# Two gate chunks at a time, half of their rows as seven block products

## The chip, the cores and the metric

The kernel runs on one NeuronCore of a Trainium2 chip. The core has five engines that run their own instruction queues in order: TensorE (PE, matrix products; its weight loads are listed apart as PEld), VectorE (DVE), ScalarE (ACT), GpSimd (POOL) and SyncE (SP, which here only issues transfers). Data lie in SBUF, 128 partitions wide; TensorE writes its sums to PSUM, eight banks of 128 x 512 float32. Transfers between HBM and SBUF run on 16 DMA engines. The metric is the device time of one execution in microseconds; lower is better.

## The reference, cut to what matters

One layer of a streaming encoder for 256 tokens of 2048 features, in float32. The part that the change touches is the mixer:

```python
proj = h @ w_in                                   # h: 256 x 2048
(rq, rk, rv, rg, gqkv, ga, gb, gz, gate_a, gate_b) = split(proj)
yr = groupnorm(retention(rope(rq), rope(rk), rv))
yr = silu(rg) * yr
yg = rmsnorm(gated_delta_rule(conv_silu(gqkv), ga, gb))
yg = silu(gz) * yg
merged = sigmoid(gate_a) * yr + sigmoid(gate_b) * yg
x = x + merged @ w_out
```

After it come cross-attention and an MLP. `rg`, `gz`, `gate_a` and `gate_b` are each 256 x 2048 = h times a 2048 x 2048 slice of `w_in`; these four products are the gate chunks.

## The kernel before, in words

**Products in two parts.** Every float32 operand of a matmul is split into a rounded half and a remainder, `hi` and `lo`, and a product is three matmuls: hi x hi, hi x lo, lo x hi. The activations h are split once (`h1`, four quads of 512 features each, a quad holding `hi` and `lo` of 4 x 128 features by 256 tokens). Weights are split as they arrive: SP loads 1 MB into `raw` (three buffers), ScalarE rounds 1024 columns of it into `whi` (L124), VectorE subtracts into `wlo` (L125). So one load is two halves, each a `whi`/`wlo` pair of 128 x 1024; there are three buffers of each. TensorE frees a buffer with its last matmul on it.

**Chunks.** A chunk (`chunk`) is 512 output columns for all 256 tokens: two PSUM tiles (128 tokens each, t = 0 and 1) from `stream_ps`, four loads (q = 0..3, 512 rows of the weights each), 4 x 4 x 2 x 3 = 96 matmuls with the activations as weights and 512 columns of `whi`/`wlo` moving (L169 to L171). Then `evac` reads the PSUM tiles: for the gates ScalarE takes silu or tanh into `gth` (L931) and VectorE multiplies into `yr` or `yg` (L937, L943).

**Groups.** The mixer runs in four groups j = 0..3 (a quarter of the features each). The main loop goes: `gdn_stream(j)` (twelve block loads, convolution, Gram matrices in `kh`/`kl`), `gdn_blocks(j)` (a triangular solve of 31 small steps on VectorE in `lw` and `tw`, stored and reloaded as `ct`), the delta-rule gates of group j-1 (`of_delta_rule`: GZ then TB), `retention(j)` (q, k, and the chunk V, scores, norm of `yr`), then the retention gates of group j (`of_retention`: RG then TA). `gdn_core(j)` is a generator of eight small steps on TensorE, VectorE, ScalarE and GpSimd; `step()` lets it go on by one between the parts of a chunk. For j > 0 it runs during the retention gates. In the fifth pass only the delta-rule gates of group 3 are left, and `take_back` splits the merged results of the first three groups in between, into the places of the quads of h that are no longer needed.

**Order.** The program's order on each engine comes from a planner that lays the instructions out by their dependencies and priorities against its own timeline; `high_priority` lifts the weight loads and splits over everything else, the gates' `evac` less far, and `issue_after` pins an instruction behind another one. On the chip each engine's queue then runs in that fixed order.

**PSUM.** Four of the eight banks belong to the chunks (`s0`, `s1`, two each), the other four are handed out in turn by `bank()` for scores, Gram matrices, transposes and the core's steps.

**A form of sums.** The MLP's second product (`with_seven`, L1232 and L1266) already computes half of its rows in blocks of two by two, as seven block products of 12 matmuls instead of eight. Sums and differences of the weights' blocks are made on VectorE (L1266), those of the activations once per group.

Of the kernel before, what the change touches and what calls it, by code (L numbers as in the profile page):

```python
# [54 lines left out]
def trunk(ctx: ExitStack, tc: tile.TileContext, x_f, mem_f, positions, lead_f, small_f, w_blocks, w_chunks, w_ga,  # L55
# [15 lines left out]
        s1 = psp.tile([P, 512], F32, name="s1", tag="s1", bufs=2)  # L71
        return s0, s1

    def bank():
        return psp.tile([P, 512], F32, name="b", tag="b", bufs=4)


    fetched, steps, latest = [], [], {}
# [587 lines left out]
    def gdn_stream(grp):  # L666
# [3 lines left out]
        for pr in range(2):  # L670
# [17 lines left out]
                r4 = mx.tile([P, 4, NT, GD], F32, name="r4", tag="r4", bufs=1)  # L688
            grams = []
            ssk, ssq = (mx.tile([P, 2, NT], F32, name=nm, tag=nm, bufs=2) for nm in ("ssk", "ssq"))  # L690
            for b in range(2):
                kh = mx.tile([P, 2, S], F32R, name="kh", tag="kh", bufs=2)
                kl = mx.tile([P, 2, S], F32R, name="kl", tag="kl", bufs=2)
                act.activation(kh, kq[:, b], AF.Copy)
                vec.tensor_sub(kl, kq[:, b], kh.bitcast(F32))
                g0, g1 = bank(), bank()
                g0v = g0.rearrange("p (a n) -> p a n", a=2)
                g1v = g1[:, 0:256].rearrange("p (a n) -> p a n", a=2)
                for n, (l, r) in enumerate(((kh, kh), (kh, kl), (kl, kh))):
                    pe.matmul(g0v, l[:, 0, 0:P], r, start=n == 0, stop=n == 2)  # L700
                for n, (l, r) in enumerate(((kh, kh), (kh, kl), (kl, kh))):
                    pe.matmul(g1v, l[:, 0, P:S], r[:, :, P:S], start=n == 0, stop=n == 2)
                grams.append((g0v, g1v))
                for t, src in enumerate((g0v[:, 0, 0:P], g1v[:, 0, :])):
                    dj = sm.tile([P, S], F32, name="dj", tag="bo", bufs=2)[:, :P]
                    vec.scalar_tensor_tensor(dj, src, 1.0, ident, op0=ALU.mult, op1=ALU.mult,
                                             accum_out=ssk[:, b, t:t + 1])
# [217 lines left out]
            vec.tensor_mul(yr[:, t, :], yr[:, t, :], gng)  # L925


    def gates():
        def gate_of(ps, f, scale):
            th = mx.tile([P, 512], F32, name="gth", tag="gth", bufs=1)  # L930
            act.activation(th, ps, f, scale=scale)  # L931
            return th

        def silu_gate(y):
            def evac(t, ps, c0, c1):
                th = gate_of(ps, AF.Silu, 1.0)
                vec.scalar_tensor_tensor(y[:, t, :], th, 0.5, y[:, t, :], op0=ALU.mult, op1=ALU.mult)  # L937
            return evac

        def sig_gate(y, other=None):  # L940
            def evac(t, ps, c0, c1):
                th = gate_of(ps, AF.Tanh, 0.5)
                vec.scalar_tensor_tensor(y[:, t, :], th, 1.0, y[:, t, :], op0=ALU.add, op1=ALU.mult)  # L943
                if other is not None:
                    vec.tensor_add(y[:, t, :], y[:, t, :], other[:, t, :])
            return evac

        def of_retention(j, yr):
            chunk(h1, cols(w_chunks, H_RG + j), silu_gate(yr))
            chunk(h1, cols(w_chunks, H_TA + j), sig_gate(yr))  # L950

        def of_delta_rule(j, yr, yg, quad, before=None):
            chunk(h1, cols(w_chunks, H_GZ + j), silu_gate(yg))
            chunk(h1, cols(w_chunks, H_TB + j), sig_gate(yg, yr), before=before, cuts=2 if before else 1)
            to_feature(lambda t, f: yg[:, t, f * P:(f + 1) * P], quad)

        return of_retention, of_delta_rule
# [10 lines left out]
    gate_retention, gate_delta_rule = gates()  # L968
    for j in range(5):
        if j < 4:  # L970
            heads, cmp_l, r4, qe4 = gdn_stream(j)
            solved = gdn_blocks(heads, cmp_l)
        if j:
# [511 lines left out]
```

## Time and profile before

| | us |
|---|---|
| median of 3 runs | 2043.6 (2042.51 to 2044.07) |
| the profiled execution | 2043.71 |
| its span, first to last instruction | 2042.0 |
| TensorE busy | 2030.0 |
| VectorE busy | 1564.4 |
| ScalarE busy | 1202.4 |
| GpSimd busy | 39.5 |
| mean DMA rate | 198 GB/s |

A row of the profile names line, engine, operation, written and read tiles, shape and count, then busy time, the mean of one in ns, and idle time before with what ended it. Busy times of TensorE are those of overlapping matmuls: each is followed from its start to its modelled end, and the next one has started long before. How fast TensorE goes is seen in the distances between starts. Stretches are in us from the span's start; the mixer's groups lie between about 270 and 1060 us.

### The profile page before, as it was taken

Reading aid. Unit: us, or ns where it says so; the run is one execution under the profiler, and the core shown is the slowest. Engines: PE = TensorE matmul, PEld = TensorE weight load, DVE = VectorE, ACT = ScalarE, POOL = GpSimd, SP = SyncE. Lnnn points to the kernel's source line nnn. Section 1 sums busy time; section 2 is a strip of 40 time slices with the busy share of each in tenths; the row PEclk is TensorE's granted clock in tenths of the full one; section 3 lists DMA queues with packets and bytes.
Section 4 is the critical chain, followed back from the end, with each engine's and each line's share of the span. In section 5 each row is a group of like instructions: output and inputs, shape, how many; then the busy total and the mean of one; then the engine's idle time right before and its main releaser. Section 6 shows DMA issues by size and latency. Waiting matters only on the chain.

```text
span 2042.0 us, 28478 instructions
## 1 busy us (share of the span) xinstructions
PE 2030.0 (99%) x10790; PEld 1751.2 (86%) x10790; DVE 1564.4 (77%) x2427; ACT 1202.4 (59%) x1979; POOL 39.5 (2%) x50
## 2 busy tenths in 40 slices
PE   9999999999999999999999999999999999999998
PEld 8888888988888888888888899888888888888886
DVE  5887788779668875788567666777887887888788
ACT  5665764575457554755446565566557656656655
POOL 0000000000000000000000000000000000000000
PEclk9999999999999999999999999999999999999999
DMA  8678556455545554555467554568636546555661
GB/s 328 210 267 290 182 185 201 157 187 193 188 170 181 193 194 164 182 188 194 146 211 251 196 176 158 183 216 277 208 130 238 215 159 220 196 203 174 238 228 62
DMA packets 79642, 405.24 MB, mean 198 GB/s; under 512 B 16512, under 2 KB 24592, under 8 KB 34832
## 3 DMA queue, kind: packets, MB, share of 16 engines
q1 hardware_dynamic: 79072, 402.74, 57.4%
q8 instruction: 84, 1.38, 0.3%
q10 hardware_dynamic: 432, 0.69, 0.1%
q14 instruction: 54, 0.44, 0.1%
HBM read 389.74 MB, written 11.55 MB: 197 GB/s over the span
## 4 chain that ended last, share of the span: by engine, by line
PE 97%; DVE 2%; issue 0%; DMA 0%; ACT 0%; DVEq 0%; POOLq 0%; POOL 0%; ACTq 0%
PE s L213 52%; PE s L170 8%; PE s L171 8%; PE s L169 8%; PE s L1232 7%; PE b L1232 7%; PE s L402 1%; PE s L403 1%; PE s L404 1%; PE b L797 1%; PE b L700 1%; PE b L141 1%; PE b L830 1%; PE b L140 1%; PE b L142 1%
## 5 line engine op out<-in xcount | busy, mean ns | idle before, releaser
L213 PE MATMUL s<-q,whi 128*128 128x512 f32 x2824 | 971.6, 391 | 0.0
L125 DVE TENSOR_TENSOR wlo<-raw,whi 128x1024 fp32r<-128x1024 f32 x599 | 730.5, 1222 | 284.0 <-ACT whi L124 279.4
L124 ACT ACTIVATE whi<-raw 128x1024 fp32r<-128x1024 f32 x599 | 635.0, 1061 | 500.2 <-PE s L213 219.1
L213 PE MATMUL s<-q,wlo 128*128 128x256 f32 x2824 | 766.1, 281 | 0.0
L213 PEld LDWEIGHTS s<-q,whi 128*128 128x128 f32 x2824 | 521.8, 188 | 100.9
L213 PEld LDWEIGHTS s<-q,wlo 128*128 128x128 f32 x2824 | 528.7, 188 | 13.1 <-DVE wlo L125 0.4
L170 PE MATMUL s<-wlo,q 128*128 128x512 f32 x704 | 277.2, 394 | 0.0
L171 PE MATMUL s<-whi,q 128*128 128x512 f32 x704 | 274.9, 391 | 0.0
L169 PE MATMUL s<-whi,q 128*128 128x512 f32 x704 | 254.4, 391 | 0.0
L169 PEld LDWEIGHTS s<-whi,q 128*128 128x128 f32 x704 | 132.1, 188 | 27.3
L171 PEld LDWEIGHTS s<-whi,q 128*128 128x128 f32 x704 | 132.3, 188 | 26.3
L170 PEld LDWEIGHTS s<-wlo,q 128*128 128x128 f32 x704 | 132.3, 188 | 26.2
L222 ACT ACTIVATE bo<-s 128x256 f32<-128x256 f32 x192 | 73.3, 382 | 109.4 <-PE s L213 109.2
L1232 PE MATMUL s<-whi,q 128*128 128x512 f32 x384 | 122.1, 389 | 0.0
L223 DVE TENSOR_TENSOR bo<-bo,s 128x256 f32<-128x256 f32 x192 | 79.9, 416 | 41.9 <-ACT bo L222 41.5
L1255 DVE TENSOR_TENSOR wlo<-rt,whi 128x1024 fp32r<-128x1024 f32 x55 | 67.4, 1226 | 35.8 <-ACT whi L1254 35.4
L213 PE MATMUL s<-q,whx 128*128 128x512 f32 x248 | 86.6, 390 | 0.0
L1232 PEld LDWEIGHTS s<-whi,q 128*128 128x128 f32 x384 | 72.1, 188 | 14.9
L1254 ACT ACTIVATE whi<-rt 128x1024 fp32r<-128x1024 f32 x55 | 58.2, 1059 | 41.8 <-PE s L1232 29.4
L1232 PE MATMUL s<-wlo,q 128*128 128x512 f32 x192 | 74.7, 389 | 0.0
L213 PE MATMUL s<-q,wlx 128*128 128x256 f32 x248 | 68.2, 280 | 0.0
L1232 PE MATMUL b<-whi,q 128*128 128x512 f32 x208 | 67.2, 389 | 0.0
(355 smaller groups left out, 2328.2 us busy)
## 6 DMA issues: line engine op xcount, KB each, us to landing
raw<-w_ff SPq DMA_DIRECT2D x96, 1024.0 KB
raw<-w_chunks SPq DMA_DIRECT2D x79, 1024.0 KB
raw<-w_blocks SPq DMA_DIRECT2D x64, 1024.0 KB
raw<-w_xk SPq DMA_DIRECT2D x16, 1024.0 KB
raw<-w_out SPq DMA_DIRECT2D x16, 1024.0 KB
raw<-w_xq SPq DMA_DIRECT2D x16, 1024.0 KB
raw<-w_xo SPq DMA_DIRECT2D x16, 1024.0 KB
rt<-w_ff SPq DMA_DIRECT2D x16, 1024.0 KB
```

Source lines behind the costliest of these rows:

```text
L124: latest["hi"] = act.activation(hi[:, cs], src[:, cs], AF.Copy).ins
L125: latest["lo"] = vec.tensor_sub(lo[:, cs], src[:, cs], hi[:, cs].bitcast(F32)).ins
L140: pe.matmul(o, lhs[0], rhs[0], start=first, stop=False)
L169: pe.matmul(o, xh, wh, start=first, stop=False)
L170: pe.matmul(o, xh, wl, start=False, stop=False)
L171: pe.matmul(o, xl, wh, start=False, stop=last)
L213: ins = pe.matmul(ps[b][:, :S] if part else ps[b], halves[h][part][:, i, b * P:(b + 1) * P], x[:, kk % 4, :], start=kk == 0 and not part, ...
L222: act.activation(o, ps[b][:, S:], AF.Copy)
L223: vec.tensor_add(o, o, ps[b][:, :S])
L1232: ins = pe.matmul(o, lhs[l], rhs[r], start=key not in opened, stop=last and j == 2, skip_group_check=True).ins
L1254: latest["hi"] = act.activation(hi, raw[:, c:c + 1024], AF.Copy).ins
L1255: latest["lo"] = vec.tensor_sub(lo, raw[:, c:c + 1024], hi.bitcast(F32)).ins
```

## The change

The gates keep their values, but four pairs of chunks are computed together by a new function, `two_chunks`: the retention gates (RG and TA) of groups 1, 2 and 3, and the delta-rule gates (GZ and TB) of group 3. Of the 2048 rows, quads 2 and 3 (`plain`) are computed as before. Rows of quads 0 and 1 are taken as a product of blocks: tokens in two halves of 128, rows in two halves of 512, and the two chunks as the two halves of the columns. Seven products of 12 matmuls (`product`) take the place of eight.

The sums on the side of the tokens are made once, into `s_in` (`sums_of_tokens`, hung into `turns`, so that they are issued after the 10th, 20th, 30th and 40th half from the start of group 1). The sums on the side of the weights are made in SBUF: x takes the block (chunk 1, quad 0) by two plain loads, VectorE adds b11 (`add_to`), GpSimd issues two transfers that add the block (1, 1) from HBM on top (`add_parts`, `accum_op`), and later two that add (0, 1); y takes (1, 0) and VectorE adds b22. Three partial sums are kept in `u` and `d` (places of `vh` and `vl`), and the gates' `evac` adds them (`more`) before the silu or tanh.

In the order of the code a pair is eleven parts: plain(0, 2), b11, x, plain(0, 3), b22, x, plain(1, 2), b21, y, x, plain(1, 3). x lies in the places of `kq` and `lw`, y in those of `qk` and `tw`. The four turning banks become two tags of two banks, `b` and `c`; during a pair `c` holds `shared` and `p5`, and the core's steps have `b` alone. The tiles `kh`, `kl` of the Gram matrices move to the places of `vh` and `vl`. The scratch space for transfers issued by GpSimd is set to 4096.

```diff
--- before.py
+++ after.py
@@ -71,8 +71,13 @@
         s1 = psp.tile([P, 512], F32, name="s1", tag="s1", bufs=2)
         return s0, s1
 
-    def bank():
-        return psp.tile([P, 512], F32, name="b", tag="b", bufs=4)
+    taken, kept_back = [0], []
+
+    def bank(tag=None):
+        if not tag:
+            taken[0] += not kept_back
+            tag = "b" if kept_back or taken[0] % 2 else "c"
+        return psp.tile([P, 512], F32, name="b", tag=tag, bufs=2)
 
 
     fetched, steps, latest = [], [], {}
@@ -688,9 +693,9 @@
                 r4 = mx.tile([P, 4, NT, GD], F32, name="r4", tag="r4", bufs=1)
             grams = []
             ssk, ssq = (mx.tile([P, 2, NT], F32, name=nm, tag=nm, bufs=2) for nm in ("ssk", "ssq"))
+            k_hl = tuple(mx.tile([P, 2, 2, S], F32R, name="k" + e, tag="v" + e, bufs=1) for e in "hl")
             for b in range(2):
-                kh = mx.tile([P, 2, S], F32R, name="kh", tag="kh", bufs=2)
-                kl = mx.tile([P, 2, S], F32R, name="kl", tag="kl", bufs=2)
+                kh, kl = (a[:, b] for a in k_hl)
                 act.activation(kh, kq[:, b], AF.Copy)
                 vec.tensor_sub(kl, kq[:, b], kh.bitcast(F32))
                 g0, g1 = bank(), bank()
@@ -925,33 +930,184 @@
             vec.tensor_mul(yr[:, t, :], yr[:, t, :], gng)
 
 
+    s_in = tuple(mx.tile([P, 4, 512], F32R, name="s" + e, tag="s" + e, bufs=1) for e in "hl")
+
+    def sums_of_tokens(i):
+
+        xs = mx.tile([P, 2, 512], F32, name="xs", tag="qk", bufs=1)
+        whole, sv = (xs[:, e, :].rearrange("p (a n) -> p a n", a=n) for e, n in ((0, 2), (1, 4)))
+        for g in range(2):
+            vec.tensor_add(whole[:, g], *(h1[g].both[:, i, c:c + S].bitcast(F32) for c in (0, S)))
+        (a11, a21), (a12, a22) = ((whole[:, g, 0:P], whole[:, g, P:S]) for g in range(2))
+        vec.tensor_sub(sv[:, 0], a21, a22)
+        vec.tensor_sub(sv[:, 1], sv[:, 0], a11)
+        vec.tensor_sub(sv[:, 2], a11, a21)
+        vec.tensor_add(sv[:, 3], a12, sv[:, 1])
+        split([a[:, i, :] for a in s_in], xs[:, 1, :])
+
+    def two_chunks(chunks, evacs, before=None):
+
+
+
+        own = [stream_ps(), stream_ps()]
+        shared, p5 = bank("c"), bank("c")
+        kept_back.append(None)
+        x, y = ([mx.tile([P, 1024], F32, name=n, tag=tag, bufs=1) for n, tag in these]
+                for these in ((("xa", "kq"), ("xb", "lw")), (("ya", "qk"), ("yb", "tw"))))
+        opened, ends = set(), []
+
+        def lines(n, q, h):
+            return w_chunks[chunks[n], q][:, h * 1024:(h + 1) * 1024]
+
+        def load_parts(to, n, q):
+            with tc.high_priority(offset=100000), tc.issue_after(fetched[-1]):
+                for h in range(2):
+                    fetched.append(nc.sync.dma_start(to[h], lines(n, q, h)).ins)
+
+        def add_parts(to, n, q):
+            with tc.high_priority(offset=100000):
+                for h in range(2):
+                    pool.dma_start(to[h], lines(n, q, h), accum_op=ALU.add)
+
+        def add_to(to, src):
+            with tc.high_priority(offset=100000):
+                for h in range(2):
+                    with tc.issue_after(latest["lo"]):
+                        vec.tensor_add(to[h], to[h], src[h])
+
+        def load(n, q):
+            raw = wp.tile([P, 4 * 512], F32, name="raw", tag="raw", bufs=3)
+            with tc.high_priority(offset=100000):
+                fetched.append(nc.sync.dma_start(raw, w_chunks[chunks[n], q]).ins)
+            return raw[:, 0:1024], raw[:, 1024:2048]
+
+        def parted(srcs):
+            halves = []
+            with tc.high_priority(offset=100000):
+                for src in srcs:
+                    hi, lo = (h[:, :1024] for h in half_tiles())
+                    latest["hi"] = act.activation(hi, src, AF.Copy).ins
+                    latest["lo"] = vec.tensor_sub(lo, src, hi.bitcast(F32)).ins
+                    halves.append([a.rearrange("p (k n) -> p k n", n=512) for a in (hi, lo)])
+            return halves
+
+        def triple(o, lhs, rhs, key):
+            for l, r in ((0, 0), (0, 1), (1, 0)):
+                with tc.issue_after(ends[-1]) if ends else ExitStack():
+                    ins = pe.matmul(o, lhs[l], rhs[r], start=key not in opened, stop=False, skip_group_check=True).ins
+                opened.add(key)
+            return ins
+
+        def product(o, lhs, srcs, key):
+            halves = parted(srcs)
+            for i in range(4):
+                ins = triple(o, lhs(i), [a[:, i % 2, :] for a in halves[i // 2]], key)
+            ends.append(ins)
+            step()
+
+        def plain(n, q):
+            halves = parted(load(n, q))
+            for i in range(4):
+                for t in range(NT):
+                    ins = triple(own[n][t], [a[:, i, t * P:(t + 1) * P] for a in h1[q]],
+                                 [a[:, i % 2, :] for a in halves[i // 2]], (n, t))
+                if i % 2:
+                    ends.append(ins)
+                    step()
+
+        def part(g, t):
+            return lambda i: [a[:, i, t * P:(t + 1) * P] for a in h1[g]]
+
+        def summed(c):
+            return lambda i: [a[:, i, c * P:(c + 1) * P] for a in s_in]
+
+        def kept_sum(tag, ps):
+            o = mx.tile([P, 2, 512], F32, name="u", tag=tag, bufs=1)
+            act.activation(o[:, 0], ps, AF.Copy)
+            return o
+
+        def finish(n, t, more):
+            with tc.high_priority(offset=50000):
+                evacs[n](t, own[n][t], 0, 512, more)
+
+        def others(q):
+            if before:
+                before(q)
+
+        plain(0, 2)
+        load_parts(x, 1, 0)
+        b11 = load(0, 0)
+        product(shared, part(0, 0), b11, "shared")
+        add_to(x, b11)
+        with tc.high_priority(offset=50000):
+            u = kept_sum("vh", shared)
+        u1, u3 = u[:, 0], u[:, 1]
+        product(p5, summed(0), x, "p5")
+        add_parts(x, 1, 1)
+        plain(0, 3)
+        load_parts(y, 1, 0)
+        b22 = load(1, 1)
+        product(own[1][0], summed(3), b22, (1, 0))
+        add_to(y, b22)
+        product(shared, summed(1), x, "shared")
+        add_parts(x, 0, 1)
+        with tc.high_priority(offset=50000):
+            d = kept_sum("vl", shared)
+        others(1)
+        plain(1, 2)
+        b21 = load(0, 1)
+        product(own[0][0], part(1, 0), b21, (0, 0))
+        finish(0, 0, u1)
+        product(shared, summed(2), y, "shared")
+        with tc.high_priority(offset=50000):
+            act.activation(u3, shared, AF.Copy)
+            vec.tensor_sub(d[:, 0], p5, d[:, 0])
+            vec.tensor_sub(d[:, 1], p5, u3)
+        product(own[0][1], part(1, 1), x, (0, 1))
+        finish(0, 1, u3)
+        others(2)
+        others(3)
+        plain(1, 3)
+        kept_back.clear()
+        for t in range(NT):
+            finish(1, t, d[:, t])
+
     def gates():
-        def gate_of(ps, f, scale):
+        def gate_of(ps, f, scale, more):
             th = mx.tile([P, 512], F32, name="gth", tag="gth", bufs=1)
+            if more is not None:
+                vec.tensor_add(th, ps, more)
+                ps = th
             act.activation(th, ps, f, scale=scale)
             return th
 
         def silu_gate(y):
-            def evac(t, ps, c0, c1):
-                th = gate_of(ps, AF.Silu, 1.0)
+            def evac(t, ps, c0, c1, more=None):
+                th = gate_of(ps, AF.Silu, 1.0, more)
                 vec.scalar_tensor_tensor(y[:, t, :], th, 0.5, y[:, t, :], op0=ALU.mult, op1=ALU.mult)
             return evac
 
         def sig_gate(y, other=None):
-            def evac(t, ps, c0, c1):
-                th = gate_of(ps, AF.Tanh, 0.5)
+            def evac(t, ps, c0, c1, more=None):
+                th = gate_of(ps, AF.Tanh, 0.5, more)
                 vec.scalar_tensor_tensor(y[:, t, :], th, 1.0, y[:, t, :], op0=ALU.add, op1=ALU.mult)
                 if other is not None:
                     vec.tensor_add(y[:, t, :], y[:, t, :], other[:, t, :])
             return evac
 
         def of_retention(j, yr):
+            if j in (1, 2, 3):
+                two_chunks((H_RG + j, H_TA + j), (silu_gate(yr), sig_gate(yr)))
+                return
             chunk(h1, cols(w_chunks, H_RG + j), silu_gate(yr))
             chunk(h1, cols(w_chunks, H_TA + j), sig_gate(yr))
 
         def of_delta_rule(j, yr, yg, quad, before=None):
-            chunk(h1, cols(w_chunks, H_GZ + j), silu_gate(yg))
-            chunk(h1, cols(w_chunks, H_TB + j), sig_gate(yg, yr), before=before, cuts=2 if before else 1)
+            if j in (3,):
+                two_chunks((H_GZ + j, H_TB + j), (silu_gate(yg), sig_gate(yg, yr)), before)
+            else:
+                chunk(h1, cols(w_chunks, H_GZ + j), silu_gate(yg))
+                chunk(h1, cols(w_chunks, H_TB + j), sig_gate(yg, yr), before=before, cuts=2 if before else 1)
             to_feature(lambda t, f: yg[:, t, f * P:(f + 1) * P], quad)
 
         return of_retention, of_delta_rule
@@ -968,6 +1124,9 @@
     gate_retention, gate_delta_rule = gates()
     for j in range(5):
         if j < 4:
+            if j == 1:
+                for i in range(4):
+                    turns.extend(9 * [lambda: None] + [lambda i=i: sums_of_tokens(i)])
             heads, cmp_l, r4, qe4 = gdn_stream(j)
             solved = gdn_blocks(heads, cmp_l)
         if j:
@@ -1446,7 +1605,7 @@
     import concourse.bacc as bacc
     from concourse.bass_utils import run_bass_kernel_spmd
 
-    nc = bacc.Bacc("TRN2", target_bir_lowering=False, num_devices=1)
+    nc = bacc.Bacc("TRN2", target_bir_lowering=False, num_devices=1, dynamic_dma_scratch_size=4096)
     arrays, args = {}, {}
     for name in _INS:
         arrays[name] = np.ascontiguousarray(inputs[name])
```

## The prediction

> **What bounds the kernel now.** I read the page first, then the ends of the chunks on ScalarE, then a table of stretches, then single rows. From the page of the kernel before (busy time, chain of waits, groups):
>
> ```profile
> span 2042.0 us, 28478 instructions
> ...
> PE 2030.0 (99%) x10790; PEld 1751.2 (86%) x10790; DVE 1564.4 (77%) x2427; ACT 1202.4 (59%) x1979; POOL 39.5 (2%) x50
> ...
> PE 97%; DVE 2%; issue 0%; DMA 0%; ACT 0%; DVEq 0%; POOLq 0%; POOL 0%; ACTq 0%
> ...
> L125 DVE TENSOR_TENSOR wlo<-raw,whi 128x1024 fp32r<-128x1024 f32 x599 | 730.5, 1222 | 284.0 <-ACT whi L124 279.4
> L124 ACT ACTIVATE whi<-raw 128x1024 fp32r<-128x1024 f32 x599 | 635.0, 1061 | 500.2 <-PE s L213 219.1
> ...
> L170 PE MATMUL s<-wlo,q 128*128 128x512 f32 x704 | 277.2, 394 | 0.0
> ```
>
> TensorE is the chain from end to end, so a matmul less is time less, as long as VectorE goes on delivering halves. The 394 ns is one matmul from start to modelled end, and they overlap; the price of one is the distance between two. The last two gate chunks, 96 matmuls each with nothing else on TensorE, end where ScalarE begins to read their sums (ScalarE rows in order of time: start, duration, line, tile):
>
> ```profile
> 1013.76 0.60 ACT L931 ACTIVATE gth<-s 128x512 f32<-128x512 f32 x1
> ...
> 1035.52 0.60 ACT L931 ACTIVATE gth<-s 128x512 f32<-128x512 f32 x1 [0.98 <-PE s L171]
> ...
> 1057.28 0.60 ACT L931 ACTIVATE gth<-s 128x512 f32<-128x512 f32 x1 [0.98 <-PE s L171]
> ```
>
> 21.76 us for 96 is **0.2267 us a matmul**. Next the four stretches that the change rewrites (retention gates of groups 1, 2, 3, then the delta-rule gates of group 3), and four others in which VectorE is nearly full; columns are length, then busy time of TensorE, weight loads, VectorE, ScalarE, GpSimd, then clock, DMA share and GB/s:
>
> ```profile
> 528.20:579.50 51.30, 51.30 (x276) 44.13 (x275) 31.02 (x56) 23.07 (x44) 3.42 (x4) 1.00 0.50 169
> 744.50:796.60 52.10, 52.10 (x279) 44.78 (x278) 30.25 (x51) 23.25 (x43) 3.30 (x3) 1.00 0.47 162
> 961.70:1013.80 52.10, 52.10 (x280) 44.75 (x279) 30.20 (x51) 23.31 (x44) 2.91 (x3) 1.00 0.46 158
> 1013.80:1057.30 43.50, 43.50 (x193) 36.02 (x192) 25.42 (x27) 21.02 (x23) 1.01 (x1) 1.00 0.55 191
> 890.00:915.00 25.00, 25.00 (x114) 20.80 (x113) 24.35 (x46) 11.73 (x13) 0.00 (x0) 1.00 0.59 191
> 1655.00:1680.00 25.00, 25.00 (x112) 20.67 (x112) 24.48 (x25) 12.77 (x12) 0.00 (x0) 1.00 0.39 135
> 1825.00:1850.00 25.00, 25.00 (x112) 20.71 (x111) 24.48 (x25) 12.76 (x12) 0.00 (x0) 1.00 0.39 133
> 1995.00:2020.00 25.00, 25.00 (x112) 20.70 (x111) 24.99 (x26) 14.33 (x17) 0.00 (x0) 1.00 0.10 39
> ```
>
> Two readings carry the forecast. In the four stretches VectorE is 58 to 60% busy, so there is room. And in the last three rows, where the MLP already runs block products of this kind, VectorE is 98 to 100% busy while TensorE starts 112 matmuls in 25 us, 0.223 us each: a full VectorE alone has not slowed TensorE.
>
> **The change part by part.** *Matmuls.* A pair of chunks had 192; half the rows gave 8 block products of 12, now 7. That is 12 x 0.2267 = 2.72 us a pair, **10.88 us** for four pairs.
>
> *VectorE and ScalarE.* What an operation costs VectorE is again the distance between starts, here around the end of a V chunk:
>
> ```profile
> 525.99 1.23 DVE L125 TENSOR_TENSOR wlo<-raw,whi 128x1024 fp32r<-128x1024 f32 x1 [0.39 <-ACT whi L124]
> 527.13 0.69 DVE L137 TENSOR_TENSOR vl<-s,vh 128x512 fp32r<-128x512 f32 x1
> 527.73 1.22 DVE L125 TENSOR_TENSOR wlo<-raw,whi 128x1024 fp32r<-128x1024 f32 x1
> 528.86 0.69 DVE L137 TENSOR_TENSOR vl<-s,vh 128x512 fp32r<-128x512 f32 x1
> ```
>
> 1.14 us for 1024 columns, 0.60 for 512 (with a PSUM source). A pair had 16 halves to split; it now has 8 for the plain parts and 14 for seven products: 6 more, 6.84 us. The two sums made by VectorE (`add_to`) are four operations of 1024, 4.56 us. The gates' additions (`more`) are four of 512 and the two subtractions into `d` two more, 3.60 us. Together 15.0 us a pair. So VectorE would be busy 46.0 of 48.6 us, 45.3 of 49.4, 45.2 of 49.4, and 40.4 of 40.8 in the delta-rule pair: 95, 92, 92 and 99%. By the rows above that is bearable, with nothing to spare in the last. ScalarE gains six halves (1.06 each) and three copies (0.60 each), 8.2 us on 21 to 23: no bound.
>
> *Order.* A full VectorE is harmless only while its queue has the splits at the right places. How late can one be? A half starts when TensorE frees one of three buffers, as in these rows of ScalarE and then of VectorE:
>
> ```profile
> 1041.64 1.06 ACT L124 ACTIVATE whi<-raw 128x1024 fp32r<-128x1024 f32 x1 [1.66 <-PE s L171]
> ```
>
> ```profile
> 1042.73 1.23 DVE L125 TENSOR_TENSOR wlo<-raw,whi 128x1024 fp32r<-128x1024 f32 x1 [1.49 <-ACT whi L124]
> 1043.87 1.22 DVE L965 TENSOR_TENSOR q<-mg,q 128x1024 fp32r<-128x1024 f32 x1
> 1045.45 1.23 DVE L125 TENSOR_TENSOR wlo<-raw,whi 128x1024 fp32r<-128x1024 f32 x1 [0.36 <-ACT whi L124]
> ```
>
> Free to ready is 1043.96 - 1041.64 = 2.32 us. Two other halves are used meanwhile: 5.44 us in a plain part (3.1 us to spare, which is why the 1.22 us at 1043.87 cost nothing), but 2 x 6 x 0.2267 = 2.72 us among products: 0.40 us to spare. An operation of 1.14 us before a split there makes TensorE wait 0.74. The tightest place is the sum x = b11 + x ahead of the second product: counted from the first matmul of a pair, the last half of b11 is split by 2.72 + 2.32 = 5.04, the first sum is there at 6.18, its half at 8.5, and TensorE wants it at 8.39. On its own that costs 0.1 us; whatever VectorE does in between comes on top. In a retention pair the norm of `yr` and the first core steps want VectorE at just this time (yet TensorE has their matmuls too, which stretches it). Bounds: 0, since the rows of the MLP show none, to three such intrusions, 2.2 us a pair. I take 0.5 for each retention pair, nearer to the MLP's rows, and 1.0 for the delta-rule pair with its 99%: **2.5 us** in all.
>
> *Adding transfers.* Two sums a pair are made by a transfer that adds into x; no row shows one. The nearest are the plain load and the trip of the small tile `ct` (queue rows of SP, then VectorE's wait, then two lines of the page):
>
> ```profile
> 513.11 0.82 SPq L776 DMA_DIRECT2D ct<-scr_t  x2
> 514.48 0.92 SPq L776 DMA_DIRECT2D ct<-scr_t  x2
> ```
>
> ```profile
> 519.67 0.22 DVE L782 COPY t<-ct 32x128 f32<-32x128 f32 x1 [3.17 <-DMA ct<-scr_t]
> ```
>
> ```profile
> GB/s 328 210 267 290 182 185 201 157 187 193 188 170 181 193 194 164 182 188 194 146 211 251 196 176 158 183 216 277 208 130 238 215 159 220 196 203 174 238 228 62
> ...
> q1 hardware_dynamic: 79072, 402.74, 57.4%
> ```
>
> Issue to use was 519.67 - 515.40 = 4.3 us for almost no bytes. 1.05 MB takes 3.2 us at the fastest slice (328 GB/s) and 8.1 at 130, the slowest before the last. So 7.5 to 12.4 us. The time there is: x is free when its first half has been split for the second product (5.44 + 2.32 = 7.8) and is wanted when the buffer for its next use frees, at the end of the second plain part (16.3): 8.5 us; for the second sum 18.6 to 29.9, 11.3 us. In a retention pair the core's steps stretch both; one step's eight matmuls take 0.81 us (TensorE rows):
>
> ```profile
> 543.09 1.00 PE L797 MATMUL b<-t,pair 128*128 128x64 f32 x8
> 543.90 0.48 PE L170 MATMUL s<-wlo,q 128*128 128x512 f32 x1
> ```
>
> Late by nothing up to 3.9 us in the delta-rule pair. I take nothing beyond its 1.0, as a load alongside is the likelier row, and keep the upper end for a rival.
>
> GpSimd issues these transfers, and each waits in its queue for x's last split. Behind it can stand the core's power `ro`, for which VectorE waits ahead of `yg` (waits in the first of the four stretches: who for whom, total, times, longest):
>
> ```profile
> POOL ro L269 <- DVE qe L850: 41.7, 2, 31.9
> ...
> DVE yg L853 <- POOL ro L269: 2.2, 2, 1.1
> ```
>
> GpSimd is idle nearly throughout, and `ro` comes twice in a stretch; if one of them meets a transfer, VectorE stops until the split ahead, up to one half (1.36 us), but a split is itself on VectorE ahead of it, so usually nothing: inside the 0.5.
>
> The Trainium skill speaks against this: by Collectives: The Full Stack (The bandwidth ceiling), an adding transfer reads two sources for what it writes and so moves at half the rate of a copy. An estimate by that page is 4.3 + 6.4 = 10.7 us, 2.2 us late in the delta-rule pair and not late elsewhere; the forecast would be about 1 us longer. No run here shows it yet.
>
> *Loads.* A pair reads 11 MB for 8, which lifts the DMA share of these stretches from 0.46-0.55 to about 0.7-0.8. The targets x and y reuse `kq`, `lw`, `qk`, `tw`; the solve's result is stored before 513.11 and the next pair starts at about 528, so SP does not stop at them. The delta-rule pair follows another pair directly: there x is free when part ten is split, 29.92 + 1.36 + 2.32 = 33.6 of 40.8 us, and its new sum begins 5.0 us into the next pair, 12 us later; at 7.5 us (4.3 + 3.2) the load, and b11's behind it on SP, fits.
>
> *Sums of tokens.* Four times two operations of 256, four of 128 and a split: about 2.6 us of VectorE each, two in each of these stretches:
>
> ```profile
> 356.00:436.00 80.00, 80.00 (x491) 71.46 (x490) 60.16 (x112) 52.03 (x120) 3.02 (x3) 1.00 0.52 176
> 436.00:478.20 42.20, 42.20 (x192) 35.03 (x191) 34.52 (x72) 24.34 (x51) 1.01 (x1) 1.00 0.57 191
> ```
>
> Both have over 7 us of room; behind them waits the solve, whose `ct` is wanted by the core at 528, 8 us after it came. Nothing. Without that room it would be 10.4 us.
>
> *Banks.* While a pair runs, the core has two PSUM banks for four. Its steps depend on one another anyway, so 0; bounds 0 to 0.8 us (one step's matmuls waiting) a retention pair, inside the 0.5 taken.
>
> **Sum.** The profiled execution took 2043.71 us (1.7 around the span). 2043.7 - 10.9 + 2.5 = **2035.3 us**; the median of 2043.6 stands 0.1 lower, which gives 2035.
>
> **The rivals.** *Nothing is late:* 2043.7 - 10.9 = 2032.8. For it: no gap on TensorE in the MLP's full stretches. Against it: 99% in the delta-rule pair, and DMA shares of 0.1 to 0.39 there where the pairs would have 0.7 or more.
> *VectorE's order eats it:* with an intrusion of 0.74 us at four of the seven products, 3.0 us a pair, the gain is gone: 2045; with two or three, 2039 to 2043. For it: 0.40 us to spare; against it: the MLP, whose products have the same three buffers and a fourth now and then.
> *The adding transfers are late* (the other side): VectorE and ScalarE run in order, so a late x stops both at its first half, and TensorE a buffer later. Place: parts six and ten of a pair's eleven. It turns the change into a loss once the eight sums are late by 10.9 / 8 = 1.4 us each on average. At 3 us each, 24 us: 2043.7 - 10.9 + 24 = 2057. For it: no row shows such a transfer, and loads of 1 MB would run beside it. Against it: 8.5 to 11.3 us of time.
>
> **How the numbers follow.** Forecast with small waits (2033.5 to 2039.5) 0.48; nothing late 0.14; VectorE's order 0.22, half of it within 0.2% of before; late transfers 0.16. Since 0.2% (4 us) is about what a measurement tells from no change: faster 0.64, within 0.2% 0.19, slower 0.17. Range: from 2031, a little under nothing late, to 2049, which takes in the order's rival and the mildest late transfers.
>
> **What would show it.** Right: 12 matmuls fewer in each of four stretches, each 2 to 2.7 us shorter, VectorE over 90% in them, distances of 0.227 us between the products' matmuls. VectorE's order: gaps on TensorE ended by `wlo` with an addition just ahead of it. Late transfers: ScalarE idle before x until a DMA. Wrong altogether: the stretches shorten and the time comes back elsewhere, in the first gate stage or behind the delta-rule pair.

## The result and the profile after

The changed kernel takes 2059.7 us (median; 2058.7 to 2060.5) where the kernel before took 2043.8 on the same chip: a ratio of 1.0078, with a 95% interval of 1.0066 to 1.0091. It is 15.9 us slower; 2035 was forecast, and 2049 was the end of the range. From the page of the kernel after (span, busy time, chain of waits):

```profile
span 2058.8 us, 28624 instructions
...
PE 2028.6 (99%) x10742; PEld 1746.9 (85%) x10742; DVE 1628.4 (79%) x2519; ACT 1235.3 (60%) x2019; POOL 54.5 (3%) x66
...
PE 92%; DVE 5%; issue 1%; DMA 1%; ACT 1%; SPq 0%; DVEq 0%; POOLq 0%; POOL 0%; ACTq 0%
```

The 48 matmuls are gone (10790 to 10742), and TensorE's share of the chain fell from 97% to 92%: VectorE holds 5% of it, for 2% before. Where the time came back is seen from the ends of the delta-rule gates of groups 0, 1 and 2, between which lies one retention pair each. ScalarE's rows of before, then of after (start, duration, line, tile):

```profile
478.21 0.60 ACT L931 ACTIVATE gth<-s 128x512 f32<-128x512 f32 x1 [0.98 <-PE s L171]
...
695.48 0.60 ACT L931 ACTIVATE gth<-s 128x512 f32<-128x512 f32 x1 [0.98 <-PE s L171]
...
912.62 0.60 ACT L931 ACTIVATE gth<-s 128x512 f32<-128x512 f32 x1 [0.98 <-PE s L171]
```

```profile
478.16 0.60 ACT L1081 ACTIVATE gth<-s 128x512 f32<-128x512 f32 x1 [0.46 <-PE s L176]
...
700.65 0.60 ACT L1081 ACTIVATE gth<-s 128x512 f32<-128x512 f32 x1 [0.98 <-PE s L176]
...
922.81 0.60 ACT L1081 ACTIVATE gth<-s 128x512 f32<-128x512 f32 x1 [0.98 <-PE s L176]
```

Up to 478 us, where the sums of tokens lie, nothing moved. From there to 700.65 it is 222.5 us instead of 217.3, and the next stretch 222.2 instead of 217.1: the two retention pairs **lost 5.2 and 5.0 us where each should have gained 2.7**, a difference of 7.9 and 7.7. The view of waits of the kernel after (who waits for whom, total, times, longest) names it at once:

```profile
PE b L997 <- DVE yr L928: 14.8, 3, 4.9
PE b L997 <- DVE wlo L990: 1.8, 2, 0.9
```

Three times, once per retention pair, a matmul of a product (L997) into a bank `b` waits 4.9 us for VectorE's normalisation of `yr` (L928). TensorE's rows there, then VectorE's, then GpSimd's:

```profile
536.17 0.97 PE L802 MATMUL b<-cu,pair 128*128 128x32 f32 x8
542.02 0.77 PE L997 MATMUL b<-whi,sh 128*128 128x512 f32 x1 [4.88 <-DVE yr L928]
542.59 0.63 PE L997 MATMUL b<-wlo,sh 128*128 128x512 f32 x1
543.01 0.63 PE L997 MATMUL b<-whi,sl 128*128 128x512 f32 x1
...
547.71 0.52 PE L997 MATMUL s<-wlo,q 128*128 128x512 f32 x1
548.07 0.62 PE L997 MATMUL s<-whi,q 128*128 128x512 f32 x2
```

```profile
531.21 1.22 DVE L976 TENSOR_TENSOR xb<-xb,raw 128x1024 f32<-128x1024 f32 x1
...
534.87 1.19 DVE L990 TENSOR_TENSOR wlo<-xa,whi 128x1024 fp32r<-128x1024 f32 x1
...
536.07 0.96 DVE L928 TENSOR_SCALAR yr<-b,mv,rg 128x256 f32<-128x256 f32 x2
536.95 1.21 DVE L990 TENSOR_TENSOR wlo<-xb,whi 128x1024 fp32r<-128x1024 f32 x1
538.09 0.15 DVE L923 TENSOR_SCALAR ve<-mv 128x2 f32<-128x2 f32 x1
...
540.88 1.00 DVE L928 TENSOR_SCALAR yr<-b,mv,rg 128x256 f32<-128x256 f32 x2
```

```profile
538.48 0.87 POOL L970 DMA_DIRECT2D xb<-w_chunks  x1 [1.04 <-DVE nu L811]
539.05 1.69 POOL L274 TENSOR_TENSOR rg<-ve,nhalf_pow 128x2 f32<-128x2 f32 x1
```

The matmul is the first into `p5`, and its first operands were split by 536.1. What it lacks is its **bank**. `p5` and `shared` take the two banks `c`, and the last holder of one of them is `ops` of `retention` for the second token tile, which is given back when L928 has read it, at 541.88. That reading is late because VectorE takes the splits of x ahead of `ve`, and because on GpSimd `rg` then stands 0.8 us behind the issue of an adding transfer (538.24 to 539.05). The second part of the loss lies behind the wait (columns as in the prediction's table of stretches):

```profile
536.50:542.00 5.50, 0.64 (x6) 0.54 (x6) 5.41 (x13) 2.80 (x6) 3.20 (x3) 0.92 0.74 127
542.00:545.00 3.00, 2.98 (x7) 2.42 (x8) 1.04 (x3) 0.00 (x0) 0.00 (x0) 0.50 0.83 187
```

After the idle the granted clock is 0.50, and matmuls start 0.427 us apart (542.59 to 543.01 and on). From 542.02 to 548.07 there are 14. At full clock the 12 of them that take sums of tokens start 0.233 us apart in this kernel and the other two 0.227, which makes 3.25 us, not 6.05: 2.8 us more. 4.9 + 2.8 = 7.7, and 0.3 us for the slower distance of 48 such matmuls makes 8.0, about the pair's difference. In the other two retention pairs the half clock cost 2.6 and 2.4 us. The Trainium skill, TensorE: Matmul & The Clock Gate (What's actually happening), puts the clock at half after an idle window of about 3.4 us; the idle here was longer, and the trace agrees. Its 426.7 ns for a 512-column matmul at half clock (Wait — 56ns, not 53.3ns?) is what these rows show.

### The profile page after: what moved, and what is told of

The parts are those of the page before. It is cut to its first block, busy times and chain, and to the rows that moved or that the text cites. A ratio compares the mean times of both kernels' runs of the same rounds, so it can differ in the third digit from the quotient of the medians.

```text
span 2058.8 us, 28624 instructions
## 1 busy us (share of the span) xinstructions
PE 2028.6 (99%) x10742; PEld 1746.9 (85%) x10742; DVE 1628.4 (79%) x2519; ACT 1235.3 (60%) x2019; POOL 54.5 (3%) x66
## 4 chain that ended last, share of the span: by engine, by line
PE 92%; DVE 5%; issue 1%; DMA 1%; ACT 1%; SPq 0%; DVEq 0%; POOLq 0%; POOL 0%; ACTq 0%
PE s L218 50%; PE s L1391 7%; PE b L1391 7%; PE s L175 5%; PE s L174 5%; PE s L176 5%; PE s L997 4%; PE b L997 2%; DVE wlo L990 1%; PE s L407 1%; PE s L408 1%; PE s L409 1%; PE b L835 1%; PE b L705 0%; DVE wlo L130 0%
## 5 line engine op out<-in xcount | busy, mean ns | idle before, releaser
L218 PE MATMUL s<-q,whi 128*128 128x512 f32 x2824 | 971.8, 391 | 0.5 <-DVE bo L228 0.5
L129 ACT ACTIVATE whi<-raw 128x1024 fp32r<-128x1024 f32 x535 | 567.4, 1061 | 429.2 <-PE s L218 217.7
L130 DVE TENSOR_TENSOR wlo<-raw,whi 128x1024 fp32r<-128x1024 f32 x535 | 651.6, 1221 | 212.9 <-ACT whi L129 208.8
L218 PE MATMUL s<-q,wlo 128*128 128x256 f32 x2824 | 765.2, 281 | 0.3 <-DVE wlo L130 0.3
L218 PEld LDWEIGHTS s<-q,whi 128*128 128x128 f32 x2824 | 521.6, 188 | 101.3 <-DVE bo L228 0.8
L218 PEld LDWEIGHTS s<-q,wlo 128*128 128x128 f32 x2824 | 528.7, 188 | 13.9 <-DVE wlo L130 0.8
L175 PE MATMUL s<-wlo,q 128*128 128x512 f32 x448 | 176.2, 393 | 0.0
L176 PE MATMUL s<-whi,q 128*128 128x512 f32 x448 | 174.6, 390 | 0.0
L174 PE MATMUL s<-whi,q 128*128 128x512 f32 x448 | 159.0, 390 | 0.0
L1391 PE MATMUL s<-whi,q 128*128 128x512 f32 x384 | 122.1, 389 | 0.0
L997 PE MATMUL s<-whi,q 128*128 128x512 f32 x320 | 101.8, 392 | 0.0
L174 PEld LDWEIGHTS s<-whi,q 128*128 128x128 f32 x448 | 83.9, 188 | 17.4
L176 PEld LDWEIGHTS s<-whi,q 128*128 128x128 f32 x448 | 84.2, 188 | 16.8
L175 PEld LDWEIGHTS s<-wlo,q 128*128 128x128 f32 x448 | 84.2, 188 | 16.7
L990 DVE TENSOR_TENSOR wlo<-raw,whi 128x1024 fp32r<-128x1024 f32 x56 | 68.1, 1222 | 28.9 <-ACT whi L989 28.5
L989 ACT ACTIVATE whi<-raw 128x1024 fp32r<-128x1024 f32 x56 | 59.2, 1058 | 46.1 <-PE b L997 25.8
L218 PE MATMUL s<-q,whx 128*128 128x512 f32 x248 | 86.6, 390 | 0.0
L1391 PEld LDWEIGHTS s<-whi,q 128*128 128x128 f32 x384 | 72.1, 188 | 15.0
```

The lines of the kernel that those rows point to most:

```text
L129: latest["hi"] = act.activation(hi[:, cs], src[:, cs], AF.Copy).ins
L130: latest["lo"] = vec.tensor_sub(lo[:, cs], src[:, cs], hi[:, cs].bitcast(F32)).ins
L174: pe.matmul(o, xh, wh, start=first, stop=False)
L175: pe.matmul(o, xh, wl, start=False, stop=False)
L176: pe.matmul(o, xl, wh, start=False, stop=last)
L218: ins = pe.matmul(ps[b][:, :S] if part else ps[b], halves[h][part][:, i, b * P:(b + 1) * P], x[:, kk % 4, :], start=kk == 0 and not part, ...
```

## The experiments

My theory was the bank. Rivals: the adding transfers, on GpSimd and in landing, hold things up (which had given 2057 in the prediction, close to the result), or VectorE's order is at fault and the bank only the place where it shows. Ratios are to the kernel before on the same chip, with 95% intervals.

**Banks apart.** In `retention`, scores and outputs get tags of their own, so that both banks `c` are free long before a pair:

```diff
-            sps = bank()
+            sps = bank("c")
...
-            ops = bank()
+            ops = bank("b")
```

> The changed kernel with the retention's PSUM banks sorted by hand: its two score tiles take the banks of tag c, its two outputs those of tag b, so that shared and p5 (tag c) follow on score tiles that are read early; the core's steps (tag b) follow on the outputs. VectorE's and GpSimd's work is the same. Theory 1 (the bank): the 4.9 us waits at the second product go; the core's second step may wait a little for the second output; 2034 to 2044. Theory 2 (adding transfers): 2056 to 2062. Theory 3 (VectorE overloaded): 2056 to 2062.

2042.4 us, 0.9998 (0.9989 to 1.0008): some 17 us less than the changed kernel. The wait for `yr` is no longer among the waits of this kernel:

```profile
PE b L997 <- DVE wlo L990: 2.9, 6, 0.9
PE s L218 <- DVE bo L228: 1.4, 1, 1.4
...
PE s L997 <- DVE wlo L990: 0.8, 1, 0.8
```

So the wait for the bank was what cost the time, and what is left costs as much as the change saves.

**VectorE in place of the adding transfers**, with the banks of the change:

```diff
         def add_parts(to, n, q):
-            with tc.high_priority(offset=100000):
-                for h in range(2):
-                    pool.dma_start(to[h], lines(n, q, h), accum_op=ALU.add)
+            add_to(to, load(n, q))
```

> The changed kernel without the transfers that add: each of the eight sums is made by a plain load into a raw buffer and two additions on VectorE (2.3 us each, 18 us of VectorE in all). GpSimd's queue is as in the kernel before. Theory 1 (the bank): the wait for p5's bank stays, at most 1.7 us shorter a pair because GpSimd is free for the power rg: 2053 to 2064. Theory 2 (adding transfers): the loss goes, 2030 to 2042. Theory 3 (VectorE overloaded): worse by up to the 18 us: 2064 to 2078.

2068.0 us, 1.0122 (1.0107 to 1.0137): above the 2064 at which my theory's range ended, and inside that of a VectorE with too much to do. Without any adding transfer the same wait is longer:

```profile
PE b L995 <- DVE yr L928: 21.6, 3, 7.2
```

The transfers are not the cause; VectorE's additional sums push L928 further back. The bank is where TensorE waits, and VectorE's queue sets for how long.

**The norm ahead.** `add_to` is pinned behind the last L928, which leaves the banks as they are but gives the one in question back early:

```diff
-                vec.tensor_scalar(yr[:, t, es], ops[:, es], ...
+                latest["norm"] = vec.tensor_scalar(yr[:, t, es], ops[:, es], ...
...
-                    with tc.issue_after(latest["lo"]):
+                    with tc.issue_after(latest["lo"]), tc.issue_after(latest["norm"]):
```

> The changed kernel with one order fixed: VectorE's additions into x and y stand behind the last normalising operation of yr (line 928 of the changed kernel) in its queue. Nothing else changes. Theory 1 (a PSUM bank: the second product's sum p5 takes the bank that the retention's second token half still holds until it is normalised, and TensorE waits 4.9 us for it in each retention pair, then runs at half clock for 2.8 us more): the wait on that bank goes, a shorter one of 1 to 2 us for the sum x takes its place, short enough to keep the clock; 24 us lost become about 5, so 2038 to 2044. Theory 2 (the transfers that add are too slow or hold up GpSimd's queue): they are the same, so 2056 to 2062. Theory 3 (VectorE is overloaded): the same work in another order, 2055 to 2062.

2054.4 us, 1.0057 (1.0040 to 1.0074): a miss for my theory, which had expected the loss to be gone. The bank's wait is gone and another stands in its place (VectorE's rows, then the waits):

```profile
533.24 1.90 DVE L928 TENSOR_SCALAR yr<-b,mv,rg 128x256 f32<-128x256 f32 x4
535.05 1.22 DVE L976 TENSOR_TENSOR xa<-xa,raw 128x1024 f32<-128x1024 f32 x1
...
538.72 1.22 DVE L990 TENSOR_TENSOR wlo<-xa,whi 128x1024 fp32r<-128x1024 f32 x1
```

```profile
PE b L997 <- DVE wlo L990: 6.5, 5, 2.0
PE b L997 <- ACT whi L989: 4.4, 2, 2.2
```

The norm ends at 535.1, and now x's halves are late, split at 538.7 instead of 534.9. Both are wanted by the same matmul at the same moment; VectorE can do only one of them first. Nor were the new waits short enough to keep the clock, as I had expected: in the first pair one of 1.99 us was, but in the second and third two waits, of 2.2 and then 1.3 or 1.5 us with one matmul between them, brought the half clock again, with 10 and 12 distances of 0.427 us (TensorE's rows of the second pair):

```profile
756.78 0.69 PE L997 MATMUL b<-whi,sh 128*128 128x512 f32 x1 [2.21 <-ACT whi L989]
758.76 0.80 PE L997 MATMUL b<-wlo,sh 128*128 128x512 f32 x1 [1.29 <-DVE wlo L990]
759.35 0.63 PE L997 MATMUL b<-whi,sl 128*128 128x512 f32 x1
759.78 0.63 PE L997 MATMUL b<-whi,sh 128*128 128x512 f32 x1
```

The rival of VectorE's order thus holds half of the truth: in the place where the change puts `p5`, neither of these two orders on VectorE serves both. An order between them, with only the small `ve` ahead of x's splits, was not run.

**The matmuls later.** If that is so, a later use of `p5` should cure it without touching banks or VectorE. In the three retention pairs `plain(0, 3)` (24 matmuls) goes ahead of the second product; `plain(1, 2)` and `plain(1, 3)` move too, so that the adding transfers keep their time (the delta-rule pair keeps its order). As it acts in a retention pair, the edit is, cut:

```diff
+        plain(0, 3)
         product(p5, summed(0), x, "p5")
         add_parts(x, 1, 1)
-        plain(0, 3)
...
+        plain(1, 2)
         product(shared, summed(1), x, "shared")
         add_parts(x, 0, 1)
...
-        plain(1, 2)
...
+        plain(1, 3)
+        for t in range(NT):
+            finish(1, t, d[:, t])
         product(own[0][1], part(1, 1), x, (0, 1))
         finish(0, 1, u3)
```

> The banks stay as in the changed kernel. In the three retention pairs the plain product of the first chunk's last block (24 matmuls, 5.4 us) is moved ahead of the second product of sums, so that the bank is asked for 5.4 us later; two other plain products are moved so that the adding transfers keep their time. If the bank that the output still holds is the cause, the wait of 4.9 us goes, the half clock behind it too, and the time is near that with the banks apart, 2041 to 2046. If VectorE's order is the cause and the bank only the place where it shows, the normalisation moves later as well and the time stays at 2054 to 2060.

2040.0 us, 0.9984 (0.9975 to 0.9993): 19.7 us off the changed kernel's time, a little better than the 2041 to 2046 expected, and faster than before. VectorE's row of the norm, then TensorE's rows of `p5`:

```profile
540.85 1.00 DVE L928 TENSOR_SCALAR yr<-b,mv,rg 128x256 f32<-128x256 f32 x2
```

```profile
542.51 0.39 PE L997 MATMUL b<-whi,sh 128*128 128x512 f32 x1
542.75 0.40 PE L997 MATMUL b<-wlo,sh 128*128 128x512 f32 x1
```

The normalisation comes at the same time as in the changed kernel (540.85 for 540.88). Nobody waits for it any more, since TensorE has 24 other matmuls to do first. That refutes the rival's version, in which the norm would only have moved later.

**The idle filled.** Is the half clock the idle's own, or do the products of sums bring it? Twenty matmuls whose result is overwritten afterwards, work that the reference doesn't have, stand where TensorE was idle; banks and order are the change's:

```diff
+        if before is None:
+            for i in range(20):
+                with tc.issue_after(ends[-1]):
+                    ins = pe.matmul(own[1][0], h1[0][0][:, 0, 0:P], s_in[0][:, i % 4, :], start=True, stop=True,
+                                    skip_group_check=True).ins
+            ends.append(ins)
         product(p5, summed(0), x, "p5")
```

> The changed kernel, with 20 matmuls of 128x512 whose result is overwritten (work that the reference doesn't have, 20 x 0.227 = 4.5 us) put where TensorE stands idle for 4.9 us in each retention pair. The theory that the low granted clock behind the idle is the idle's own expects the distance of the matmuls behind it to stay at 0.23 us, and the time 2 to 2.8 us less in each pair, 2051 to 2054, though no wait is taken away. The rival, that the low clock belongs to the products of sums (their operands or banks), expects the matmuls behind to keep 0.427 us, and 2059 to 2061.

2051.8 us, 1.0042 (1.0028 to 1.0056). Sixty matmuls more make the kernel 7.9 us faster than the changed one. TensorE's rows (L1048 is the added work):

```profile
537.10 3.52 PE L1048 MATMUL s<-sh,q 128*128 128x512 f32 x14
540.46 0.47 PE L997 MATMUL b<-whi,sh 128*128 128x512 f32 x1
540.77 0.39 PE L997 MATMUL b<-wlo,sh 128*128 128x512 f32 x1
541.00 0.39 PE L997 MATMUL b<-whi,sl 128*128 128x512 f32 x1
...
543.33 0.39 PE L997 MATMUL s<-whi,q 128*128 128x512 f32 x1
```

541.00 to 543.33 are ten distances, 0.233 each and not 0.427: the idle brings the half clock. The added matmuls take about as long as the wait did, so the 7.9 us are the half clock's: 2.6 us a pair, as the 2.8, 2.6 and 2.4 us in the changed kernel's rows.

**The delta-rule pair alone**: the retention gates are chunks again.

```diff
         def of_retention(j, yr):
-            if j in (1, 2, 3):
+            if j in ():
```

> The new form for the delta-rule pair of group 3 alone; the retention gates of groups 1 to 3 are computed as before (the sums of tokens are still made). This pair has the fullest VectorE (99 percent by my sum) and two of the eight adding transfers' sums, but no retention ahead of it whose banks are held. Theory 1 (the bank): nothing of the loss is here; 2.7 us gained less 2.4 us of waits for halves read in the trace: 2042 to 2045. Theory 2 (adding transfers): a quarter of the loss of 27 us less 2.7: 2047 to 2049. Theory 3 (VectorE overloaded): most of it is here: 2050 or more.

2044.0 us, 1.0003 (0.9994 to 1.0013), as expected: its 2.7 us are lost again. TensorE's waits for halves in this pair come to 1.4 us, the slower distance to 0.3; the rest isn't located. **The retention pairs alone**, with the banks apart:

```diff
         def of_delta_rule(j, yr, yg, quad, before=None):
-            if j in (3,):
+            if j in ():
```

> Retention's score sums and outputs have banks that the pair doesn't take, and the delta-rule pair is two chunks again; three retention pairs stay. With the banks apart, the three pairs together came to about -2 us of 36 matmuls less (8.2 us) and the delta-rule pair to about +1. The theory of the banks expects 2040 to 2042.5, below the kernel before by 1 to 3 us. The rival, that whatever the pair saves goes to VectorE's order anywhere in the gates, expects no difference from before, 2043 to 2044.

2040.4 us, 0.9985 (0.9976 to 0.9994), as expected. The same with the second parts of x's sums on VectorE (the edit of `add_parts` above):

> Banks apart, no delta-rule pair, and the second parts of both sums by loads and VectorE's sums in place of the adding transfers: 4 sums of 1024 elements more on VectorE in each retention pair, of about 1.1 us each. With the bank's wait gone, the theory of the banks expects that these cost only where VectorE sets the time: 0 to 1.5 us a pair, 2041 to 2046. If the adding transfers themselves cost something (their landing, or GpSimd held while it issues them), it is faster than the kernel with transfers.

2045.8 us, 1.0012 (1.0003 to 1.0021), 5.5 us more, 1.8 a pair, a little above what was expected. With the bank out of the way, VectorE's additions show as waits for halves:

```profile
PE b L995 <- DVE wlo L988: 4.9, 3, 1.6
```

So the adding transfers do take work off VectorE that would cost time. **Banks apart, moved matmuls, retention pairs only:**

> Banks apart, the moved plain products, and no delta-rule pair. The theory of the banks: nothing is left that the order of products could cure but the waits for halves of 0.3 to 0.8 us, so 2038.5 to 2042, equal to or a little below the same kernel without the moved products. The rival of VectorE's order expects the moved products to matter by themselves: 2 us or more below it.

2039.3 us, 0.9981 (0.9972 to 0.9990), as expected. **The moved matmuls and retention pairs only**, with the change's banks:

> The banks of the changed kernel, the moved plain products in the three retention pairs, and two chunks in place of the delta-rule pair. The retention pairs each came to -2.1 us with the moved products; the delta-rule pair, by its waits, cost 3.8 us and saved 2.7. The theory that the delta-rule pair now costs about 1 us expects 2037.5 to 2039.5; the rival, that it is neutral as it was alone, expects 2040, no change from the kernel with it.

2037.2 us, 0.9967 (0.9955 to 0.9980), the fastest here: 6.4 us below before, 22.5 below the change, and 0.3 below the expected range. One of its gate stretches, and the ends of its delta-rule gates:

```profile
528.20:579.50 51.30, 51.28 (x275) 43.72 (x274) 43.98 (x70) 31.44 (x53) 9.81 (x10) 1.00 0.63 183
```

```profile
693.03 0.60 ACT L1090 ACTIVATE gth<-s 128x512 f32<-128x512 f32 x1 [0.98 <-PE s L176]
...
908.05 0.60 ACT L1090 ACTIVATE gth<-s 128x512 f32<-128x512 f32 x1 [0.98 <-PE s L176]
```

215.0 us between them where before had 217.1: **2.1 us for a pair with nothing late**. VectorE is 86% busy there.

## Why the prediction was wrong

*Banks: the step that failed.* "While a pair runs, the core has two PSUM banks for four ... so 0; bounds 0 to 0.8 us." I asked who is left with fewer banks and not who held the pair's own two, and until when. The price was 14.8 us of wait in three pairs and 2.8, 2.6 and 2.4 us of half clock behind it, 22.6 us of the 24.7 between forecast and result. Smaller terms add to it: 0.233 us for a matmul of a product of sums (48 a pair, 0.3 us a pair, 1.2 in all), 1.8 us of waits in the delta-rule pair, and a wait of 0.5 at L218 behind it. The 2.5 us of waits that the forecast already held go off again. That makes 23.6; the last 1.1 us is not located.

*Order: half right.* I wrote that the norm of `yr` and the core's first steps "want VectorE at just this time", and priced that as a delay of x's splits. In the change the splits went first, the norm came late, and the norm held a bank. The norm-ahead experiment shows the other side: with the norm first, x's halves are the late ones (waits of up to 2.2 us, two in a row in two of the pairs). The bound of 2.2 us a pair had no room for the half clock.

*Matmuls: right, a little too much.* 48 fewer, and 2.1 us a pair, not 2.72, where nothing waits. 0.3 of the missing 0.6 is the slower distance; the rest isn't located. VectorE's 15.0 us more a pair were too much as well: about 13 in the gate stretch shown last (43.98 us for 31.02 before).

*The delta-rule pair: too small.* I took 1.0 us of waits. The kernel after has 1.8 for `wlo` (the row above) and 0.5 at L218, with VectorE without a pause around the first of these waits:

```profile
1034.00:1042.00 8.00, 7.07 (x32) 5.49 (x31) 8.00 (x8) 6.13 (x8) 1.76 (x2) 1.00 0.72 247
```

Over the whole pair (1031.2 to 1074.8 us) VectorE was busy 38.3 of 43.6 us, 88% and not the 99% of the forecast; the first wait comes where its work is bunched. "A full VectorE alone has not slowed TensorE" was read from the MLP and does not carry over, though there too VectorE makes differences between the splits (its row of before):

```profile
1656.15 2.35 DVE L1266 TENSOR_TENSOR rt<-tr,rt 128x1024 f32<-128x1024 f32 x2
```

The MLP's products also use the buffers `whx` and `wlx`, which a pair has not; whether that is the reason was not tried. Alone this pair is neutral. Beside the three retention pairs with the moved matmuls, leaving it out brought 2.8 us, and 2.0 with the banks apart. In the first of these kernels TensorE's waits in the pair and behind it are 3.8 us against 2.7 saved, which explains 1.1, or 1.4 with the slower distance. The rest stays open.

*Adding transfers: right in the retention pairs.* I put them at 7.5 to 12.4 us against 8.5 and 11.3 us of time. Issues of GpSimd in the kernel after (KB each, median us from issue to landing):

```profile
xa<-w_chunks POOLq DMA_DIRECT2D x8, 512.0 KB, 6.5
xb<-w_chunks POOLq DMA_DIRECT2D x8, 512.0 KB, 9.5
```

From the first issue to the last landing, the two transfers of a sum took 8.1 to 12.1 us. In the retention pairs ScalarE waits for none of them. In the delta-rule pair they are a little late: in the changed kernel ScalarE waits 1.1 us for `xb` (until 1049.31), and TensorE does not wait behind it. The Trainium skill's half rate for a sum of two sources (Collectives: The Full Stack, The bandwidth ceiling, where it is measured on a ReduceScatter) gave the estimate of 10.7 us, which lies among these times; with other loads running alongside they do not show the rate itself. The rival of late transfers came within 3 us of the result by luck: its mechanism took no part in the loss. It costs something in the delta-rule pair with the banks apart, where TensorE then waits 0.8 us for the late half, at 1050.18 (ScalarE's waits in 1005 to 1085 us of that kernel):

```profile
ACT whi L989 <- DMA xb<-w_chunks: 4.6, 2, 3.1
```

*GpSimd's queue: incomplete.* I looked behind the transfers for `ro` alone and took nothing for it; `rg`, the reciprocal root of the norm, is on the same engine and lost 0.8 us there.

*Sums of tokens, loads: right.* The delta-rule gates before the first pair end at 478.16 for 478.21, and no wait for a load shows in the gates.

## What to carry to other kernels

When an edit reserves PSUM banks, find for each the last tile that it held and the instruction that reads that tile last; the new owner's first matmul waits there, and with it everything behind it on TensorE. If that reader sits on an engine that the same edit loads, try letting other matmuls go first before you reorder the busy engine; here that took 19.7 us off, other banks 17.3, the other order 5.3. A wait of TensorE that is long enough to lower its clock is to be priced with the slow matmuls behind it, here 4.9 us and 2.4 to 2.8 more.

## What the runs showed of the hardware

- An idle stretch of 4.9 us brought the granted clock down to 0.50, with 0.427 us between 512-column matmuls instead of 0.227, for 5 to 6 us. In the norm-ahead kernel a wait of 1.99 us left the distance behind it at 0.23 us (TensorE's rows there), but two waits of 2.2 and 1.3 us with one matmul between them brought 0.427 us (its rows of the second pair, above):

```profile
539.99 0.50 PE L997 MATMUL b<-wlo,sh 128*128 128x512 f32 x1 [1.99 <-DVE wlo L990]
540.33 0.39 PE L997 MATMUL b<-whi,sl 128*128 128x512 f32 x1
540.56 0.40 PE L997 MATMUL b<-whi,sh 128*128 128x512 f32 x1
```

- In the pairs, matmuls of 512 columns with the sums of tokens (`s_in`) as weights start 0.233 us apart, those with plain activations 0.227. It is not the sums as such: in the MLP of the kernel before, 12 matmuls with sums as weights take 2.72 us (1658.68 to 1661.40), 0.227 each. Nor is it the side: in the idle-filled kernel the added matmuls, which have plain activations as weights and `s_in` moving, mostly start 0.232 to 0.235 us apart. Why is open.
- Adding transfers of 512 KB into SBUF landed 6.5 and 9.5 us after their issue (medians), with plain loads beside them.
